# Index scores of three blocks summed by sign diagonals on TensorE, with the threshold search and the value GEMM beside them

## The chip, the cores and the metric

The kernel runs on one core of a Trainium2 chip. The metric is the device time of one execution in microseconds (us). A core has five engines with queues of their own: TensorE (PE; its weight loads are listed as PEld), VectorE (DVE), ScalarE (ACT), GpSimd (POOL) and SyncE (SP, which issues the DMA transfers). An engine works its queue off in order. They wait for each other through semaphores alone.

## What is computed

The program is a two-layer decoder trunk in float32 on 1,040 positions (16 meta tokens and 1,024 tokens, width 1,024). The change touches the first layer's sparse attention. For each block of 128 queries an indexer scores all earlier keys, the 256 best keys of each query stay, and grouped attention (16 query heads, 4 key heads) runs over them:

```
q, k, v, qi, ki, wi = split(h @ w_in)         # 1024, 256, 256, 512, 64, 8 columns
logits = einsum('qhd,sd->qhs', qi_blk, ki)    # 8 index heads of 64
score  = einsum('qh,qhs->qs', w_blk, relu(logits))
score  = where(causal, score, -inf)
_, idx = top_k(score, 256)                    # per query row
s = einsum('qgrd,qkgd->qgrk', q_blk, k[idx]) * scale ; p = softmax(s) ; o = p @ v[idx]
```

After it come the output projection, an MLP, a second attention layer over a shared key and value set, and another MLP. They are the same before and after.

## The kernel before

**Index scores.** A block b of 128 queries has L[b] = 144 + 128 b keys: 272, 400, 528, 656, 784, 912, 1,040 for b = 1 to 7 (block 0 keeps all its keys). `scores(b)` (L452) walks over 8 heads and, in each, over chunks of at most 400 keys: two matmuls (L458, L459; operand format float32r, high and low part of the key) make the logits in a PSUM bank of the tag `pt`, ScalarE takes relu times the absolute head weight (L461, tile `tm`), and VectorE multiplies by the sign of the weight and adds to the score row `sc` (L463 for head 0, L465 for the others). For b = 5, 6, 7 these are 2, 3 and 3 chunks times 8 heads, 64 pieces. Over all of them the moving columns are 8 x (784 + 912 + 1,040) = 21,888.

**Threshold search.** `threshold(b0, b1)` (L483) finds each row's 256th value bit by bit: 31 bits, and in a bit one count per block. VectorE counts blocks 1, 2, 5 and 7 (L481, a comparison with an accumulator); ScalarE counts 3, 4 and 6 (L498, Sign with an accumulator). Then three small VectorE operations form the next candidate `cand` (L500, L503, L504), for which the next bit's counts wait. After the bits there is a last count, and one `mask` (L521) for each block: a count, a comparison (L526), a scan (L527), two combining operations (L529, L531) and two GpSimd operations. `thr1` searches blocks 1 to 4 (37 steps), `thr2` blocks 5 to 7 (36 steps).

**GEMMs.** `a_gemm` (through `gemm_c`, L192) makes K in 2 and Q in 8 slices of 128 columns. A slice has three chunks of some 346 positions, a chunk 24 matmuls (L199). Each K chunk goes through a head norm (L264: ScalarE L269, L279, L284; a float32 matmul L274; VectorE L286 to L292) and through `rope` (L355: four DMAs, three GpSimd operations). A Q chunk takes two ScalarE copies (L437 and one at L141) and rope. `gemm_v` (L213) makes V in 9 windows of 24 matmuls with 256 columns (L220). The copied pieces lie in a ring `raw` of five tiles (L375).

**Stages.** `weave` (L226) hands out the steps of several generators in proportion to their weights: first scores of 5 to 7, the K GEMM and 4 steps of `thr1` (L558); then 29 steps of `thr1`, 16 of `thr2` and the Q GEMM (L561); then the last 4 of `thr1` and V (L563). After that comes the attention of this layer: `unit(b, g)` makes logits (L671), their biased minimum on VectorE (L674) and the exponential (L699). `pv_stream` (L713) transposes the probabilities (L725) two units later and multiplies them with V. `WHOLE` (L707) says for each block how many of 8 such products are done in one float32 matmul (L745, recorded as two); the others are split into a high and a low float32r part (a VectorE subtraction at L148, two matmuls at L748). One step of `thr2` goes with each unit of blocks 0 to 4 (L767). The weave is no fixed order: when the program is built, a scheduler orders each engine's queue, with the order of the weave as priority, and lets an operation whose inputs it expects earlier go ahead.

## Time and profile before

| | us |
|---|---|
| median of three runs | 2957.9 (2950.74 to 2958.91) |
| profiled execution, its own time | 2962.78 |
| span of the trace in it | 2960.6 |
| TensorE busy | 2727.7 (92%) |
| VectorE busy | 2092.8 (71%) |
| ScalarE busy | 1485.5 (50%) |
| GpSimd busy | 1307.6 (44%) |

The busy times are sums over the whole program, whose stages have different limits. The change lies in the first quarter: scores of the large blocks with K at about 131 to 190 us, Q to 314, V to 352, attention of blocks 0 to 4 from 358 to 525, of blocks 5 to 7 to 686. Everything after that, three quarters of the time, is the same code in both. In the rows below "x" counts instructions, a mean is in ns, and a granted clock of 1.00 is 2.4 GHz, 0.50 is 1.2 GHz. A float32 matmul is recorded as two instructions.

### The profile page before, as it was taken

The page shows a single profiled execution, that of the slowest core. Times are in us where ns is not written, and L with a number is a line of the kernel's source. Part 1 is how long each engine was busy: PE and PEld are TensorE (multiplying, and loading weights), DVE is VectorE, ACT ScalarE, POOL GpSimd, SP SyncE. Part 2 cuts the span into 40 slices and gives each one's busy share as a digit, 9 for nine tenths or more (in the row PEclk, how much of TensorE's full clock was granted, in tenths as well). Part 3 has the DMA queues.
Part 4 walks back from the last instruction along what each step waited for, and adds up shares of the span by engine and source line. Part 5 has one row for each costly group of instructions (what it writes and reads, how often), then busy time and mean ns, then how long its engine had stood idle before and what let it go on. Part 6 is the DMA issues. An engine that isn't in the chain of part 4 may idle for free.

```text
span 2960.6 us, 45611 instructions
## 1 busy us (share of the span) xinstructions
PE 2727.7 (92%) x16570; PEld 2384.1 (81%) x16570; DVE 2092.8 (71%) x3802; ACT 1485.5 (50%) x2828; POOL 1307.6 (44%) x1199
## 2 busy tenths in 40 slices
...
GB/s 170 79 46 73 53 16 1 1 1 99 81 80 158 144 144 187 144 123 131 152 63 59 51 51 51 51 51 51 102 58 68 116 162 149 152 185 150 150 134 73
DMA packets 243154, 281.92 MB, mean 95 GB/s; under 512 B 22273, under 2 KB 183873, under 8 KB 242929
## 3 DMA queue, kind: packets, MB, share of 16 engines
...
## 4 chain that ended last, share of the span: by engine, by line
PE 58%; DVE 22%; DMA 7%; ACT 5%; POOL 4%; issue 4%; SPq 0%; DVEq 0%; POOLq 0%; ACTq 0%
PE ac L986 32%; PE ps L186 6%; PE ps L199 6%; DMA ld<-rdr 5%; DVE sc L481 4%; PE ps L671 2%; PE ps L1330 2%; PE ps L725 2%; PE ps L745 2%; PE ps L1308 2%; PE ps L1276 1%; PE ps L748 1%; DVE sc L465 1%; DVE opa L148 1%; DVE opc L148 1%
## 5 line engine op out<-in xcount | busy, mean ns | idle before, releaser
L986 PE MATMUL ac<-opc,g 128*128 128x260 f32 (+1 forms) x3456 | 580.4, 324 | 33.3 <-ACT q L141 11.5
L986 PEld LDWEIGHTS ac<-opc,g 128*128 128x128 f32 x3456 | 504.9, 191 | 92.7 <-issue 13.4
L986 PE MATMUL ac<-opb,g 128*128 128x260 f32 (+1 forms) x2304 | 389.6, 325 | 55.1 <-ACT opb L141 38.2
L986 PEld LDWEIGHTS ac<-opb,g 128*128 128x128 f32 x2304 | 336.8, 191 | 99.0 <-ACT opb L141 43.8
L986 PE MATMUL ac<-opa,g 128*128 128x260 f32 (+1 forms) x2304 | 394.6, 324 | 1.3 <-ACT g L141 0.8
L986 PEld LDWEIGHTS ac<-opa,g 128*128 128x128 f32 x2304 | 340.3, 191 | 37.2 <-ACT g L141 1.0
L978 POOL TENSOR_TENSOR t<-rb,t 128x512 f32<-128x512 f32 x128 | 191.4, 1495 | 338.4 <-DMA rb<-in_mlp_w_dram 288.7
L148 DVE TENSOR_TENSOR g<-t,g 128x512 fp32r<-128x512 f32 x256 | 225.9, 882 | 132.0 <-ACT g L141 129.6
L141 ACT ACTIVATE g<-t 128x512 fp32r<-128x512 f32 x256 | 161.1, 629 | 264.9 <-PE ac L986 166.9
L199 PE MATMUL ps<-xhb,wh 128*128 128x256 f32 (+5 forms) x640 | 207.4, 324 | 5.0 <-DVE z L1138 2.9
L199 PE MATMUL ps<-xhb,wl 128*128 128x256 f32 (+5 forms) x640 | 196.6, 307 | 0.0
L199 PE MATMUL ps<-xlb,wh 128*128 128x256 f32 (+5 forms) x640 | 196.4, 307 | 0.0
L978 POOL TENSOR_TENSOR t<-ra 128x512 f32<-128x512 f32 x64 | 96.3, 1504 | 177.1 <-DVE g L148 172.0
L1290 POOL TENSOR_SCALAR bp<-bp,bnm 128x400 f32<-128x400 f32 (+7 forms) x128 | 108.5, 858 | 143.8 <-DVE bnm L1288 143.6
L148 DVE TENSOR_TENSOR g<-rb,g 128x512 fp32r<-128x512 f32 x128 | 114.6, 896 | 57.0 <-ACT g L141 56.9
L671 PE MATMUL ps<-ks,qs 128*128 128x512 f32 (+4 forms) x448 | 130.0, 396 | 20.8 <-DVE qs L602 12.5
L141 ACT ACTIVATE bth<-ps 128x512 fp32r<-128x512 f32 (+4 forms) x224 | 110.9, 498 | 60.8 <-PE ps L1308 54.6
L199 PEld LDWEIGHTS ps<-xhb,wh 128*128 128x128 f32 x640 | 121.9, 190 | 23.6 <-issue 9.3
L141 ACT ACTIVATE q<-ac 128x520 f32<-128x520 f32 (+1 forms) x96 | 57.6, 600 | 165.4 <-PE ac L986 163.0
L1330 PE MATMUL ps<-bth,bvs 128*128 128x512 f32 (+2 forms) x420 | 135.6, 399 | 3.5 <-DVE qb L1337 2.7
L148 DVE TENSOR_TENSOR bth<-ps,bth 128x512 fp32r<-128x512 f32 (+4 forms) x210 | 119.1, 568 | 26.0 <-ACT bth L141 24.7
L1267 POOL TENSOR_SCALAR bp<-bcb,cq 128x144 f32<-128x144 f32 (+7 forms) x128 | 101.3, 794 | 77.7 <-DMA bcb<-cdr 47.7
...
## 6 DMA issues: line engine op xcount, KB each, us to landing
...
```

What stands on the lines that cost most here:

```text
L141: nc.scalar.activation(dst, src, AF.Copy, scale=scale)
L148: (nc.gpsimd if pool else nc.vector).tensor_tensor(lo, src, f32(hi), OP.subtract)
L186: nc.tensor.matmul(o[0:n, 0:m], a[:, k, 0:n], b[:, k, s:s + m], start=(k == 0 and j == 0), stop=(k == NK - 1 and j == 2))
L199: nc.tensor.matmul(o[0:n, 0:m], a[:, k, 0:n], b[:, k, s:s + m], start=(k == 0 and j == 0), stop=(k == NK - 1 and j == 2))
L481: nc.vector.tensor_scalar(eqb[:, 0:L[b]], scs(b), th, None, op, OP.add, accum_out=dst[:, b:b + 1])
L671: nc.tensor.matmul(o, qs[:, h, :], kc, start=(v == 0), stop=(v == 1))
L725: nc.tensor.transpose(pt[0:rows, j * n:j * n + n], pr[j][q0:P, c0:c0 + rows], ident[q0:P, q0:P])
L978: nc.gpsimd.tensor_tensor(t, a, c, OP.subtract)
L986: nc.tensor.matmul(t[:, i, 0:m], a[:, j, :], c[:, j, o:o + m], start=start and j == 0 and v == 0, stop=stop and j == 3 and v == 2, skip_gr ...
L1267: nc.gpsimd.tensor_scalar(pj, cb[:, 0:n], 1.0, cq[:, b, h:h + 1], OP.mult, OP.add)
L1290: nc.gpsimd.tensor_scalar(pr[i], pr[i], nm[:, 3, i:i + 1], 0.0, OP.mult, OP.add)
L1330: nc.tensor.matmul(po[:, j0 * P:], v_kb, th[0:rows, v, j0 * P:], start=(kb == 0 and v == 0), stop=(kb == last and v == 1))
```

## The change

Scores of blocks 5, 6 and 7 come from a new `scores_pe`. For each block GpSimd builds eight diagonal matrices `dg` that hold the signs of the weights, with one affine_select of 128x1024. Chunks are now the outer loop and heads the inner one. For each head TensorE makes the logits as before, ScalarE the relu as before, and TensorE then adds the head into a PSUM bank with a float32 matmul of `dg` and `tm`, two heads later. At a chunk's end ScalarE copies the sum to `sc`; in a block's last chunk VectorE adds the causal triangle to the last 128 columns. The 64 operations of L463 and L465 of these blocks are gone.

Beside these scores now run K, the whole V GEMM and 30 steps of `thr1`; beside Q run the other 7 of `thr1`, its masks among them, and 26 steps of `thr2`. The third weave is gone. The `raw` ring has four tiles, which makes room for `dg`. In blocks 5 to 7 no product of probabilities and V is whole any more: 24 of 96 were, 18 of them with 512 columns.

```diff
-THR_Q = 16
-T1 = 4
+THR_Q = 26
+T1 = 30
...
-            return iw.tile([P, HWID], F32, tag="raw", name=f"raw_{name}_{s}", bufs=5)
+            return iw.tile([P, HWID], F32, tag="raw", name=f"raw_{name}_{s}", bufs=4)
...
+        def scores_pe(b):
+
+            sb = scs(b)
+            t0 = NMETA + P * b
+            dg = iw.tile([P, IH, P], F32, tag="dg", name=f"dg{b}", bufs=1)
+            sg = wsg[:, b].rearrange("p (h o) -> p h o", o=1).to_broadcast([P, IH, P])
+            nc.gpsimd.affine_select(out=dg, in_=sg, pattern=[[0, IH], [-1, P]], compare_op=OP.is_equal, fill=0.0,
+                                    base=0, channel_multiplier=1)
+            for s, m in chunks_of(L[b]):
+                acc = bank("ps")
+                tms = {}
+
+                def add(h):
+                    nc.tensor.matmul(acc[:, 0:m], dg[:, h], tms.pop(h)[:, 0:m], start=h == 0, stop=h == IH - 1)
+                for h in range(IH):
+                    o = bank("pt")
+                    nc.tensor.matmul(o[:, 0:m], s3[:, h, t0:t0 + P], kih[:, s:s + m], start=True, stop=False)
+                    nc.tensor.matmul(o[:, 0:m], s3[:, h, t0:t0 + P], kil[:, s:s + m], start=False, stop=True)
+                    tms[h] = tm = iw.tile([P, 400], F32, tag="tm", name=f"tm{b}_{h}_{s}", bufs=3)
+                    nc.scalar.activation(tm[:, 0:m], o[:, 0:m], AF.Relu, scale=wab[:, b, h:h + 1])
+                    if h > 1:
+                        add(h - 2)
+                    if h < IH - 1:
+                        yield
+                add(IH - 2)
+                add(IH - 1)
+                e = m - P if s + m == L[b] else m
+                if e > 0:
+                    copy(sb[:, s:s + e], acc[:, 0:e])
+                if e < m:
+                    nc.vector.tensor_tensor(sb[:, s + e:s + m], acc[:, e:m], trifar, OP.add)
+                yield
...
-        weave((chain(*[scores(b) for b in range(5, NB)]), 12),
-              (chain(*[a_gemm(QW + mi * P, P, k_evac(mi), fine=True) for mi in range(2)]), 18),
+        weave((chain(*[scores_pe(b) for b in range(5, NB)]), 64),
+              (chain(*[a_gemm(QW + mi * P, P, k_evac(mi), fine=True) for mi in range(2)],
+                     gemm_v(w_in, QW + KW, xh, xl, v_evac)), 27),
               (islice(thr1, T1), T1))
-        weave((islice(thr1, 33 - T1), 33 - T1), (islice(thr2, THR_Q), THR_Q),
+        weave((thr1, 37 - T1), (islice(thr2, THR_Q), THR_Q),
               (chain(*[a_gemm(mi * P, P, q_evac(mi), fine=True) for mi in range(QW // P)]), 72))
-        weave((thr1, 4), (gemm_v(w_in, QW + KW, xh, xl, v_evac), 9))
...
-        WHOLE = (6, 6, 6, 6, 6, 2, 2, 2)
+        WHOLE = (6, 6, 6, 6, 6, 0, 0, 0)
```

The scheduler's order decides where the steps of the search come to stand. On VectorE, just ahead of the attention, the queue before has bits of `thr2` (784 and 1040 are the counts of blocks 5 and 7), the last V split, and then the key and query stacks `ks` and `qs`, with the first attention operation (L674) in the last row:

```order
L503 TENSOR_TENSOR dlt<-cnt,lim 128x3
L504 SCALAR_TENSOR_TENSOR cand<-dlt,flip 128x3
L500 TENSOR_SCALAR flip<-cand 128x3
L481 TENSOR_SCALAR sc,cnt<-sc,cand 128x784
L148 TENSOR_TENSOR wl_6810<-wr_6808,wh_6809 128x1024
L481 TENSOR_SCALAR sc,cnt<-sc,cand 128x1040
L148 TENSOR_TENSOR va<-ps_3578,va 16x4x64
L148 TENSOR_TENSOR ks_3643<-ka,ks_3643 64x272 x4
L602 TENSOR_TENSOR qs_3641<-qa,qs_3641 64x8x128
L603 TENSOR_TENSOR qs_3641<-qa,qs_3641 64x8x128
L148 TENSOR_TENSOR ks_3643<-ka,ks_3643 64x240 x2
L674 ISA pb_3630,nm_0_3661<-ps_3662,sc,s_99 128x144
```

At the same place the changed queue has the last mask's last operation (1040, L564, which was L531), the scales `s` of the logits, and then the same stacks:

```order
L564 SCALAR_TENSOR_TENSOR sc<-sc,cand 128x1040
L255 TENSOR_TENSOR s_99<-s_99 128x144
L148 TENSOR_TENSOR wl_7055<-wr_7053,wh_7054 128x1024
L256 TENSOR_TENSOR s_99<-s_99 128x144
L257 TENSOR_SCALAR s_99<-s_99 128x144
L258 TENSOR_TENSOR s_99<-s_99 128x144
L602 TENSOR_SCALAR s_99<-s_99 128x144
L603 TENSOR_SCALAR s_99<-s_99 128x144
L656 MEMSET pm 16x384
L148 TENSOR_TENSOR ks_3725<-ka,ks_3725 64x272 x4
L635 TENSOR_TENSOR qs_3723<-qa,qs_3723 64x8x128
L636 TENSOR_TENSOR qs_3723<-qa,qs_3723 64x8x128
```

So the changed queue holds all 31 bits of `thr2`, its last count and its three masks ahead of the first attention operation, and none behind it. The queue before holds 20 of the 31 bits there (19 whole ones and the counts of the 20th); the other 11, the last count and the masks stand between attention operations. Of `thr1`'s 31 bits, 4 stood in the queue ahead of the end of the large blocks' scores; now 29 do.

On TensorE, where the large blocks' scores begin, the queue before has only logits (`ps<-kih,qis`) between GEMM matmuls:

```order
L199 MATMUL ps_1342<-xh,wl_1338 128x348
L458 MATMUL ps_1352<-kih,qis 128x392
L459 MATMUL ps_1352<-kil,qis 128x392
L458 MATMUL ps_1358<-kih,qis 128x392
L459 MATMUL ps_1358<-kil,qis 128x392
L458 MATMUL ps_1364<-kih,qis 128x392
```

The changed queue adds a diagonal matmul (`tm`, `dg`) two heads behind the logits, so TensorE now waits there for ScalarE's `tm`:

```order
L487 MATMUL ps_1372<-kih,qis 128x392
L488 MATMUL ps_1372<-kil,qis 128x392
L199 MATMUL ps_1357<-xh,wh_1352 128x348
L484 MATMUL ps_1338<-tm_0_0_1342,dg_1336 128x392
L487 MATMUL ps_1385<-kih,qis 128x392
L488 MATMUL ps_1385<-kil,qis 128x392
L484 MATMUL ps_1338<-tm_1_0_1370,dg_1336 128x392
L199 MATMUL ps_1357<-xl,wh_1352 128x348
```

On ScalarE in the middle of these scores, the queue before has relus (L461) and a piece of a head norm:

```order
L461 ACTIVATE tm_5_696_1951<-ps_1948,wab 128x344
L269 ACTIVATE sc<-ps_1890 128x346
L461 ACTIVATE tm_6_0_1973<-ps_1970,wab 128x348
L461 ACTIVATE tm_6_348_1979<-ps_1976,wab 128x348
L461 ACTIVATE tm_6_696_1985<-ps_1982,wab 128x344
L461 ACTIVATE tm_7_0_1991<-ps_1988,wab 128x348
L461 ACTIVATE tm_7_348_1997<-ps_1994,wab 128x348
```

The changed queue has Sign counts of blocks 3 and 4 (L531, which was L498), which wait for VectorE's `cand`, between the relus (L490), and a copy of the summed scores (L141):

```order
L531 ACTIVATE sc,cnt<-sc,cand 128x656
L141 ACTIVATE sc<-ps_1725 128x304
L531 ACTIVATE sc,cnt<-sc,cand 128x528
L490 ACTIVATE tm_0_608_1861<-ps_1858,wab 128x304
L490 ACTIVATE tm_1_608_1873<-ps_1870,wab 128x304
L269 ACTIVATE sc<-ps_1798 128x346
L490 ACTIVATE tm_2_608_1886<-ps_1883,wab 128x304
L531 ACTIVATE sc,cnt<-sc,cand 128x656
L490 ACTIVATE tm_3_608_1899<-ps_1896,wab 128x304
L490 ACTIVATE tm_4_608_1905<-ps_1902,wab 128x304
```

## Rows read from the trace of the kernel before

**Rows 1.** Busy time of each engine in stretches of the span: the columns are the stretch in us, its length, PE, PEld, DVE, ACT and POOL busy us with instruction counts, the mean granted clock of TensorE, the DMA share and GB/s.

```profile
131.00:190.00 59.00, 50.85 (x287) 44.68 (x287) 58.70 (x124) 45.44 (x100) 20.29 (x17) 1.00 0.13 34
190.00:352.00 162.00, 142.46 (x908) 139.13 (x906) 156.03 (x400) 100.25 (x220) 85.43 (x89) 0.90 0.21 54
358.00:390.00 32.00, 26.52 (x89) 17.24 (x90) 24.59 (x82) 21.99 (x67) 13.99 (x21) 0.50 0.22 51
390.00:430.00 40.00, 36.43 (x166) 21.80 (x165) 35.71 (x112) 30.04 (x83) 14.27 (x22) 0.68 0.05 13
430.00:480.00 50.00, 47.11 (x252) 32.42 (x250) 44.57 (x124) 43.23 (x102) 23.28 (x29) 1.00 0.00 1
480.00:525.00 45.00, 39.34 (x183) 26.49 (x184) 39.21 (x75) 28.89 (x61) 22.53 (x24) 0.89 0.00 1
525.00:686.00 161.00, 156.90 (x872) 115.31 (x871) 119.50 (x260) 121.11 (x241) 59.29 (x54) 1.00 0.01 1
```

**Rows 2.** Groups of VectorE instructions by line, 131 to 192 us: the sums of the scores.

```profile
L465 DVE SCALAR_TENSOR_TENSOR sc<-tm,wsg,sc 128x304 f32<-128x304 f32 (+3 forms) x56 | 34.1, 653 | 0.0
...
L463 DVE TENSOR_SCALAR sc<-tm,wsg 128x304 f32<-128x304 f32 (+3 forms) x8 | 4.7, 591 | 0.0
```

**Rows 3.** Instructions of TensorE in order of time (start us, us until the last one ends): two neighbouring float32r matmuls of V with 256 columns; then in the attention one whole product (a float32 matmul of 512 columns, two records), what follows it, one split product (two float32r matmuls of 512 columns), and what follows that.

```profile
310.73 0.28 PE L220 MATMUL ps<-wl,xh 128*128 128x256 f32 x1
310.85 0.28 PE L220 MATMUL ps<-wh,xh 128*128 128x256 f32 x1
...
642.87 1.02 PE L745 MATMUL ps<-th,va 128*128 128x512 f32 x2
643.73 0.60 PE L725 MATMUL ps<-ident,pb 128*128 128x128 f32 x4
644.09 0.71 PE L748 MATMUL ps<-th,va 128*128 128x512 f32 x2
644.64 0.62 PE L671 MATMUL ps<-ks,qs 128*128 128x512 f32 x2
```

**Rows 4.** Groups of ScalarE instructions by line, 131 to 192 us: the Sign counts of the search and the reads of their accumulators.

```profile
L498 ACT ACTIVATE sc<-sc,cand 128x528 bf16<-128x528 f32 (+1 forms) x10 | 7.9, 792 | 1.9 <-DVE cand L504 1.9
...
L498 ACT ACTIVATION_READ_ACCUMULATOR sc<-sc,cand 128x1 f32 x9 | 1.8, 202 | 0.0
```

**Rows 5.** VectorE in order of time: in the Q stage the two counts of a `thr1` bit, and two of the small operations; near the end of V the first count of a `thr2` bit and the first count of the next one.

```profile
201.73 0.48 DVE L481 TENSOR_SCALAR_CACHE_REDUCE sc<-sc,cand 128x272 f32<-128x272 f32 x1
...
202.26 0.63 DVE L481 TENSOR_SCALAR_CACHE_REDUCE sc<-sc,cand 128x400 f32<-128x400 f32 x1
...
202.81 1.33 DVE L503 TENSOR_TENSOR dlt<-cnt,lim 128x3 int32<-128x3 f32 x1
...
205.06 0.85 DVE L500 TENSOR_SCALAR flip<-cand 128x3 int32<-128x3 int32 x1
...
343.20 1.02 DVE L481 TENSOR_SCALAR_CACHE_REDUCE sc<-sc,cand 128x784 f32<-128x784 f32 x1
...
346.14 1.02 DVE L481 TENSOR_SCALAR_CACHE_REDUCE sc<-sc,cand 128x784 f32<-128x784 f32 x1
```

**Rows 6.** Groups of VectorE instructions by line, 190 to 352 us: the three small operations of the search, the weight splits and the V splits.

```profile
L504 DVE SCALAR_TENSOR_TENSOR cand<-dlt,flip 128x4 int32<-128x4 int32 (+1 forms) x47 | 20.2, 430 | 1.6
L503 DVE TENSOR_TENSOR dlt<-cnt,lim 128x4 int32<-128x4 f32 (+1 forms) x46 | 17.7, 384 | 0.5 <-ACT sc L498 0.2
L500 DVE TENSOR_SCALAR flip<-cand 128x4 int32<-128x4 int32 (+1 forms) x47 | 16.2, 346 | 1.5
...
L148 DVE TENSOR_TENSOR wl<-wr,wh 128x1024 fp32r<-128x1024 f32 x3 | 4.1, 1380 | 0.0
L148 DVE TENSOR_TENSOR va<-ps,va 128x256 fp32r<-128x256 f32 x8 | 3.3, 414 | 0.0
```

**Rows 7.** Who waited for whom (us in total, times, longest): two waits of TensorE at 131 to 190 us, one of ScalarE at 190 to 352 us.

```profile
PE ps L458 <- DVE ln L287: 5.8, 5, 3.1
...
PE ps L458 <- ACT tm L461: 2.3, 4, 1.2
...
ACT sc L498 <- DVE cand L504: 43.8, 25, 4.5
```

**Rows 8.** Groups of VectorE instructions by line, 358 to 525 us, those of the search: counts, scan, the two combining operations, the comparison, and one candidate update at the end of the bits.

```profile
L481 DVE TENSOR_SCALAR_CACHE_REDUCE sc<-sc,cand 128x784 f32<-128x784 f32 (+2 forms) x28 | 32.3, 1154 | 0.2
...
L527 DVE TENSOR_TENSOR_SCAN sc<-sc 128x784 f32<-128x784 f32 (+2 forms) x3 | 6.2, 2057 | 0.0
...
L531 DVE SCALAR_TENSOR_TENSOR sc<-sc,cand 128x784 f32<-128x784 f32 (+2 forms) x3 | 4.6, 1518 | 0.0
...
L529 DVE SCALAR_TENSOR_TENSOR sc<-sc,cnt 128x784 f32<-128x784 f32 (+2 forms) x3 | 3.7, 1248 | 0.0
...
L526 DVE TENSOR_SCALAR sc<-sc,cand 128x784 f32<-128x784 f32 (+2 forms) x3 | 2.1, 699 | 0.0
...
L514 DVE CUSTOM_DVE_ANT_0 cand<-cand,one 128x6 uint16<-128x6 uint16 x1 | 1.9, 1852 | 0.0
```

**Rows 9.** VectorE in order of time: the last split of V, and the first operation of the attention.

```profile
352.52 0.41 DVE L148 TENSOR_TENSOR va<-ps,va 16x256 fp32r<-16x256 f32 x1
...
358.08 0.37 DVE L674 CUSTOM_DVE_ANT_0 pb<-ps,sc,s 128x144 f32<-128x144 f32 x1
```

**Rows 10.** VectorE by line, 525 to 686 us: the subtraction of the split products.

```profile
L148 DVE TENSOR_TENSOR th<-ps,th 128x512 fp32r<-128x512 f32 (+1 forms) x75 | 48.1, 655 | 17.6 <-ACT th L141 16.9
```

## The prediction

> **What bounds the kernel now.** I read the busy time by stretch first [rows 1]. While the large blocks' scores run (131 to 190 us) VectorE is busy for 58.7 of 59.0 us, and through Q and V (190 to 352) for 156.0 of 162. TensorE is idle for 8 and 20 us there, ScalarE for 14 and 62. So VectorE sets the end of these two stretches. In the attention of blocks 0 to 4 (358 to 525) no engine is full: VectorE is busy for 144.1 of 167 us (24.6, 35.7, 44.6 and 39.2), TensorE for 149.4 (26.5, 36.4, 47.1 and 39.3). The latter runs partly at a low clock: the granted clock is 0.50 in the first 32 us, 0.68 in the next 40, then 1.00 and 0.89. In blocks 5 to 7 (525 to 686) TensorE is busy for 156.9 of 161 us at 1.00 and is the bound. I count from 131 us to the start of the attention, from there to block 5, and then the tail; the rest of the program is unchanged.
>
> **Stage 1, scores with K, V and most of `thr1`.** It loses VectorE's 34.1 + 4.7 = 38.8 us of sums [rows 2]. TensorE gets them back as float32 matmuls. Its sum goes by moving columns. A float32r matmul of 256 columns is followed by the next one 0.12 us later [rows 3], 0.469 ns a column. K has 6 chunks x 24 x 347 = 49,920 columns, the logits 2 x 21,888 = 43,776, V 9 x 24 x 256 = 55,296: 148,992 columns, 69.9 us. A float32 product of 512 columns occupies TensorE from 642.87 to 643.73 [rows 3], 1.68 ns a column: 36.8 us for the 21,888 columns of the diagonals and 3.5 us for the six head norms (2,080). Sum **110 us**.
>
> ScalarE: the 45.4 us of the old stretch [rows 1] hold nearly all relus, K's head norms and 10 Sign counts. 29 bits of two counts are 58, so 48 more at 0.79 + 0.20 [rows 4], 47.5 us. V's nine splits, two weight copies and eight copies of sums are 19 operations of at most about 0.79: up to 15, taken as 8. Sum 101. VectorE: 58.7 - 38.8, plus 25 more bits at about 2.25 (1.08 for both counts, from 201.73 to 202.81 [rows 5], and 0.43 + 0.38 + 0.35 for the small ones [rows 6]), plus V's 6: 82 us, no longer full.
>
> So TensorE sets this stage, with ScalarE close behind, and a diagonal matmul now waits for ScalarE's relu, whose queue also holds Signs that wait for `cand`. Behind that matmul stand the next logits and the GEMMs. The trace has TensorE waiting 5.8 + 2.3 = 8.1 us in the old stage [rows 7]; I add that much: **118 us**, between 110 and 135 (every wait of ScalarE below exposed as well). It ends at 249.
>
> Small edits cost nothing by their cover. The three sign tables stand on GpSimd behind rope, and the first diagonal stands two heads (118 / 64 x 2 = 3.7 us) behind its block's first logits; the nearest row is VectorE's split of the same 128x1024 at 1.38 us [rows 6]; uncovered, three times twice that would be 8 us, inside the bounds. Four raw tiles hold four chunks of some 6 us each in the next stage. On SP the two weight loads of V pass Q's; the DMA share is 0.13 and 0.21 [rows 1].
>
> A rule weighed against this: the product of 512 float32 columns takes 0.86 us here [rows 3]. The Trainium skill (TensorE: Matmul & The Clock Gate, section "Back-to-back issue gap") gives a gap of columns / 2.4 + 2.5 ns for a matmul and no dearer one for float32. By that the 64 diagonals would be an estimate of 64 x 145 ns = 9.3 us and stage 1 would fall to ScalarE's 101; the row speaks against it.
>
> **Stage 2, Q with the rest of the search.** The weave's numbers leave 10 steps of `thr2` to the attention, but VectorE's queue has every bit and mask ahead of the first attention operation, so all of it must end first. From the 156.0 us of 190 to 352 [rows 1] I take 25 bits of `thr1` (56) and V's splits and their weights (3.3 + two of 1.38 [rows 6], 6). I add 11 bits of `thr2` at 3.5 (38.5), and the last count and masks: scan 6.2, combining 4.6 + 3.7, comparison 2.1, update 1.9, six counts at 1.154 [rows 8], 25.4. Two counts (2 us) go before the end of stage 1. Sum **156 us**; I take **154**, since old leftovers of scores and K sit in the 156.0. The price of 3.5: one bit with nothing beside it takes 2.94 (343.20 to 346.14 [rows 5]), of which the counts are about 2.4 (1.02 for 784 elements, to scale for 1,824) and the small operations 0.55. Their means over the stage sum to 1.16, and single ones reach 1.33 and 0.85 between GpSimd's ropes [rows 5, 6]. Bounds: 2.94 and 3.6 for all 31 bits, 137 to 160. Q's own matmuls (8 x 24 x 1,040 columns x 0.469 = 94 us) lie beside it; the queues tie them to the search through ScalarE.
>
> It ends at 403. From V's last split to the first attention operation pass 5.6 us [rows 9], so the attention starts at 409 and not at 358: **+51**.
>
> **The attention of blocks 0 to 4** loses the search: of VectorE's 144.1 us, 32.3 + 6.2 + 4.6 + 3.7 + 2.1 + 1.9 = 50.8 in the large rows alone [rows 8]. What is late next is TensorE. Its busy time at the lower of the two levels is worth 26.5 x 0.50 + 36.4 x 0.32 + 39.3 x 0.11 = 29 us if all were granted at 2.4 GHz, and its idle time is 17.6. The ends are 0 (TensorE's own chain rules and stays slow) and 47 us. The first 32 us show TensorE busy at 0.50 while VectorE has room, so I expect the start to stay slow: 14 of the idle time and 13 of the clock, **-27**.
>
> **The tail.** 18 products go from 0.86 to 0.55 us (644.09 to 644.64 [rows 3]): -5.6. VectorE gets 18 x 0.66 = 12 us more [rows 10] on 119.5 of 161. I take **-5**, between -6 and +6.
>
> **Sum**: 51 - 27 - 5 = **+19 us**. The profiled execution took 2962.8 us (span 2960.6), so 2982 there; it lies 4.9 above the median, which gives **2977**.
>
> **Rivals.**
> A, on the other side: GpSimd's interference leaves VectorE. The ropes spread over a longer stage, a bit costs 2.94 and without the wait inside it about 2.8, so stage 2 loses 31 x 0.7 = 22 us, the masks some 4, and stage 1, whose TensorE waits come mostly from VectorE's late head norms (5.8 of 8.1 us), runs in 110: 19 - 22 - 4 - 8 = -15, hence **2943**. It needs a bit under 2.95 to turn the sign. For it: fewer small operations (33 triples against 47). Against: GpSimd's work per chunk is the same.
> B: the attention gives all of its 47 us back, because VectorE's pauses were what kept TensorE slow: 19 - 20 = -1, **2957**. For it: 1.00 at 430 to 480. Against: 0.50 with VectorE 77% busy.
> C: stage 1 runs in lockstep. ScalarE waits 43.8 us for `cand` in the old Q stage [rows 7]; if such waits hold up relus and with them TensorE, and its clock falls to the lower level for a part, the stage takes 150: **3009**. For it: relus and Signs alternate in the queue. Against: two relus lie in most gaps.
> D: a float32 pass costs what the rule above says: 118 falls to 101, **2960**. Only the page speaks for it.
> That the search is not moved is no rival: the queues show it.
>
> **How the numbers follow.** Forecast 0.58, A 0.12, B 0.14, C 0.12, D 0.04. The forecast's own range, from the bounds of the four terms added as independent ones (about 10, 11, 12 and 5 us), is 2957 to 2997. Below 0.3% (9 us) a measurement of this kernel can't tell from no change. Faster: A and a little of B, 0.15. Same: the rest of B, D and the forecast's lowest tenth, 0.25. Slower: the rest, 0.60. To hold 8 in 10 the range goes halfway into A and to the start of C: 2946 to 3004.
>
> **What would show it.** Right: stage 1 near 118 us with TensorE nearly full and VectorE idle by a third; the first attention operation near 409; VectorE full ahead of it and TensorE with gaps; blocks 0 to 4 in about 140 us; the tail some 5 us shorter. Wrong: a stage 1 beyond 135 (C); 31 bits at less than 3 us each (A); blocks 0 to 4 near 120 (B). Attention operations ahead of the masks would overturn the whole sum.

## The result, and the profile after

The changed kernel takes 2999.5 us (median of 4 runs, 2998.38 to 3003.04), the kernel before beside it 2958.4 (2950.74 to 2959.56): a ratio of 1.0142, 95% interval 1.0122 to 1.0163, so about 41 us slower. The profiled executions have spans of 2996.4 and 2960.6 us.

Three marks on VectorE serve for every kernel below: A, the first attention operation; B, the first biased minimum of block 5 (784 wide), where blocks 0 to 4 end; C, the first split for the output projection, where the tail ends. Behind C stands the same code everywhere; it took between 2264.8 and 2276.6 us over the profiles here, with no order in it, so parts are compared by the marks (whose start, at 131 us, itself moves by some us between executions) and whole kernels by their ratio.

| | A | A to B | B to C | C | C to the end |
|---|---|---|---|---|---|
| before | 358.1 | 169.9 | 157.8 | 685.9 | 2274.7 |
| changed | 423.1 | 153.0 | 154.6 | 730.6 | 2265.7 |

Up to C the change costs 44.8 us; 9.0 of it don't show in the spans, because the unchanged rest of this execution was that much shorter.

Busy time by stretch in the changed kernel, in the columns of [rows 1]: the scores with K, V and 29 bits of `thr1`; Q with the rest of the search; the preparation of the attention; blocks 0 to 4 in four pieces; the tail.

```profile
131.00:245.00 114.00, 109.65 (x613) 90.84 (x612) 72.62 (x255) 93.58 (x220) 21.95 (x23) 1.00 0.08 20
245.00:411.00 166.00, 126.70 (x717) 124.31 (x715) 158.40 (x312) 67.09 (x129) 89.59 (x87) 0.80 0.21 55
411.00:423.00 12.00, 1.13 (x4) 0.93 (x4) 10.16 (x14) 5.11 (x10) 6.32 (x7) 0.50 0.34 90
423.00:455.00 32.00, 26.36 (x100) 17.42 (x101) 20.44 (x77) 22.77 (x68) 14.21 (x21) 0.50 0.21 50
455.00:495.00 40.00, 35.80 (x188) 23.98 (x188) 22.58 (x81) 28.25 (x81) 15.93 (x24) 0.80 0.01 1
495.00:545.00 50.00, 49.41 (x265) 34.74 (x263) 30.08 (x83) 41.16 (x98) 26.95 (x30) 1.00 0.00 1
545.00:576.00 31.00, 29.60 (x161) 20.49 (x159) 17.31 (x42) 23.15 (x50) 13.22 (x14) 1.00 0.00 1
576.00:731.00 155.00, 148.69 (x855) 114.49 (x854) 127.96 (x281) 120.02 (x236) 56.53 (x53) 0.99 0.01 1
```

TensorE is nearly full in the first (109.65 of 114) and VectorE in the second (158.40 of 166; in [rows 1] it was full in both). In the preparation TensorE has 1.13 us of work. Blocks 0 to 4 begin with 32 us at 0.50, as before, and then TensorE is nearly full at 0.80 and 1.00 while VectorE has room.

The search in the second stretch, by line of VectorE, as in [rows 6]: the counts, then the three small operations.

```profile
L514 DVE TENSOR_SCALAR_CACHE_REDUCE sc<-sc,cand 128x784 f32<-128x784 f32 (+4 forms) x80 | 86.6, 1082 | 1.5
L536 DVE TENSOR_TENSOR dlt<-cnt,lim 128x3 int32<-128x3 f32 (+1 forms) x33 | 13.5, 408 | 3.3 <-ACT raw_q L141 0.5
...
L533 DVE TENSOR_SCALAR flip<-cand 128x3 int32<-128x3 int32 (+1 forms) x32 | 11.5, 360 | 0.9
L537 DVE SCALAR_TENSOR_TENSOR cand<-dlt,flip 128x3 int32<-128x3 int32 (+1 forms) x33 | 11.0, 332 | 0.9
```

Who waited for whom from 245 to 423 us, as in [rows 7]:

```profile
ACT sc L531 <- DVE cand L537: 65.2, 26, 5.2
POOL sc L565 <- DVE sc L564: 30.4, 6, 9.4
...
PE ps L447 <- ACT sc L437: 26.2, 7, 5.7
...
PE ps L704 <- DVE qs L635: 23.8, 1, 23.8
```

ScalarE waits 65.2 us for `cand` (43.8 in the Q and V stretch before), and behind its Signs stand Q's copies: TensorE waits 26.2 us for those. GpSimd waits 30.4 us for masks. TensorE waits 23.8 us for the first query stack (L704), before which it last had Q.

What came last ahead of A, in GpSimd's order of time: the last mask's two operations, then the last rotation of Q.

```profile
413.47 1.06 POOL L565 TENSOR_SCALAR sc<-sc 128x1040 f32<-128x1040 f32 x1
414.62 0.45 POOL L566 TENSOR_TENSOR sc<-sc,tri 128x128 f32<-128x128 f32 x1
415.03 0.86 POOL L361 TENSOR_TENSOR rotq<-rotq,rs 128x346 f32<-128x346 f32 x1
415.86 0.79 POOL L362 TENSOR_TENSOR raw_q<-raw_q,rc 128x346 f32<-128x346 f32 x1
416.73 0.91 POOL L363 TENSOR_TENSOR qa<-raw_q,rotq 128x346 f32<-128x346 f32 x1
```

And ScalarE's next two operations, the key and query stacks, with what released the first:

```profile
417.68 1.78 ACT L141 ACTIVATE ks<-ka 64x272 fp32r<-64x272 f32 x4 [8.08 <-POOL qa L363]
419.48 2.13 ACT L141 ACTIVATE qs<-qa 64x1024 fp32r<-64x1024 f32 x2
```

The last mask leaves VectorE at 410.5, but Q's last rotation stood behind its two GpSimd operations and ends at 417.6; only then do the stacks begin, and the attention 5.4 us after that.

### The profile page after: what moved, and what is told of

Same layout as the page of the kernel before. It is cut to its first block, busy times and chain, and to the rows that moved or that the text cites. A ratio compares the mean times of both kernels' runs of the same rounds, so it can differ in the third digit from the quotient of the medians.

```text
span 2996.4 us, 45902 instructions
## 1 busy us (share of the span) xinstructions
PE 2751.3 (92%) x16698; PEld 2413.5 (81%) x16698; DVE 2058.9 (69%) x3762; ACT 1490.2 (50%) x2836; POOL 1317.2 (44%) x1202
## 4 chain that ended last, share of the span: by engine, by line
PE 61%; DVE 17%; ACT 6%; DMA 6%; POOL 4%; issue 4%; SPq 0%; DVEq 0%; ACTq 0%; POOLq 0%
PE ac L1019 32%; PE ps L199 7%; PE ps L186 6%; DMA ld<-rdr 5%; DVE sc L514 3%; PE ps L704 2%; PE ps L1363 2%; PE ps L758 2%; PE ps L1341 2%; PE ps L1309 2%; PE ps L781 2%; PE ps L778 1%; DVE g L148 1%; DVE opa L148 1%; DVE opc L148 1%
## 5 line engine op out<-in xcount | busy, mean ns | idle before, releaser
L1019 PEld LDWEIGHTS ac<-opc,g 128*128 128x128 f32 x3456 | 505.6, 192 | 88.5 <-ACT q L141 12.8
L141 ACT ACTIVATE g<-t 128x512 fp32r<-128x512 f32 x256 | 161.1, 629 | 265.0 <-PE ac L1019 154.4
L704 PE MATMUL ps<-ks,qs 128*128 128x512 f32 (+4 forms) x448 | 129.0, 392 | 26.7 <-DVE qs L635 23.8
L141 ACT ACTIVATE bth<-ps 128x512 fp32r<-128x512 f32 (+4 forms) x224 | 111.3, 499 | 59.9 <-PE ps L1341 53.6
L141 ACT ACTIVATE q<-ac 128x520 f32<-128x520 f32 (+1 forms) x96 | 57.6, 600 | 165.7 <-PE ac L1019 163.3
L141 ACT ACTIVATE wh<-wr 128x1024 fp32r<-128x1024 f32 (+1 forms) x84 | 87.4, 1041 | 103.8 <-PE ps L186 70.7
```

Of the source, the lines that this page charges most:

```text
L141: nc.scalar.activation(dst, src, AF.Copy, scale=scale)
L704: nc.tensor.matmul(o, qs[:, h, :], kc, start=(v == 0), stop=(v == 1))
L1019: nc.tensor.matmul(t[:, i, 0:m], a[:, j, :], c[:, j, o:o + m], start=start and j == 0 and v == 0, stop=stop and j == 3 and v == 2, skip_gr ...
```

## The experiments

All marks and times, where a ratio was measured with its 95% interval (to the kernel before on the same chip), else the time of one execution. e7 and e12 compute the scores less precisely and e8 and e11 leave Q unrotated: they price a term and are no candidates.

| | A | A to B | B to C | time |
|---|---|---|---|---|
| e1 scores only | 393.5 | 166.8 | 153.6 | 1.0080 [1.0050, 1.0109] |
| e2 weave only | 417.6 | 147.2 | 154.6 | 1.0110 [1.0087, 1.0133] |
| e3 V last | 417.0 | 147.2 | 153.6 | 1.0088 [1.0064, 1.0112] |
| e4 block 7 | 383.7 | 160.0 | 153.6 | 1.0033 [1.0019, 1.0048] |
| e5 gate | 401.1 | 171.1 | 153.4 | 1.0118 [1.0093, 1.0143] |
| e6 gate, mixed | 396.0 | 171.6 | 153.5 | 1.0122 [1.0098, 1.0146] |
| e7 one pass | 423.3 | 150.7 | 153.5 | 2995.0 |
| e8 less rotation | 404.1 | 151.8 | 154.6 | 2979.8 |
| e9 block 7, gate | 384.3 | 171.1 | 153.8 | 1.0064 [1.0046, 1.0083] |
| e10 masks off GpSimd | 420.0 | 151.9 | 153.9 | 2994.9 |
| e11 before, less rotation | 345.3 | 170.0 | 157.8 | 2947.4 |
| e12 gate, one pass | 389.6 | 171.3 | 153.4 | 2984.4 |
| e13 gate, no Sign | 388.3 | 180.6 | 153.4 | 3000.7 |
| e14 ring and split | 358.2 | 169.0 | 153.5 | 0.9979 [0.9964, 0.9993] |
| e15 fill | 370.7 | 169.3 | 158.1 | 1.0008 [0.9994, 1.0022] |
| e16 fill and split | 370.1 | 164.7 | 153.6 | 0.9986 [0.9972, 1.0000] |
| e17 no queue ties | 388.5 | 182.4 | 153.5 | 2995.0 |

**The two halves apart.** In the diffs of the weaves here, K GEMM and Q GEMM stand for the chains of `a_gemm` that the change's diff shows. e1 is the changed kernel with the old order:

```diff
-THR_Q = 26
-T1 = 30
+THR_Q = 16
+T1 = 4
...
+        weave((chain(*[scores_pe(b) for b in range(5, NB)]), 64), (K GEMM, 18), (islice(thr1, T1), T1))
+        weave((islice(thr1, 33 - T1), 33 - T1), (islice(thr2, THR_Q), THR_Q), (Q GEMM, 72))
+        weave((thr1, 4), (gemm_v(w_in, QW + KW, xh, xl, v_evac), 9))
```

> The changed kernel with the old weaves: the three blocks' scores on TensorE, but K alone beside them with 4 bits of thr1, V last again, and (by the order of VectorE's queue) 21 of 31 bits of thr2 ahead of the attention, the rest and the masks inside it. Theory 1 (TensorE's added columns lengthen the stage in which it is nearly full, and VectorE cannot use the time that it is given): the large scores take 84 to 92 us instead of 59, Q and V stay at about 162 because VectorE stays full there, the first attention operation comes at about 387 instead of 358, the attention of blocks 0 to 4 stays at 170; about 2984 us. Rival (the sums leave VectorE for little, and only the moved search costs): the large scores stay near 65 us, VectorE takes the search earlier, the attention starts at 358 or before; 2955 us or less.

e2 has the new order with VectorE's sums:

```diff
-        weave((chain(*[scores_pe(b) for b in range(5, NB)]), 64),
+        weave((chain(*[scores(b) for b in range(5, NB)]), 12),
```

> The changed kernel with the three blocks' scores summed on VectorE as before: the new weaves, the four raw tiles and the split products alone. Theory 1: VectorE is full in the first stage, 58.7 us of old work and 25 more bits of thr1 at 2.25 and V's splits, so that stage takes about 121 us against the changed kernel's 114, the rest is as in the changed kernel; about 3006 us, so the sign diagonals gain some 7 us within the new weave. Rival (the diagonals cost more on TensorE than the sums on VectorE whatever stands beside them): the stage takes 100 us or less and the kernel 2985 us.

Each half alone loses: at B e1 is 32.3 us late and e2 36.7, both together 48.0. The first stretches, of e1 and then of e2:

```profile
131.00:215.00 84.00, 82.55 (x393) 64.96 (x392) 23.59 (x65) 51.89 (x111) 20.20 (x20) 1.00 0.08 20
215.00:393.00 178.00, 150.34 (x942) 147.52 (x940) 165.69 (x409) 105.84 (x226) 86.34 (x90) 0.86 0.21 56
```

```profile
131.00:234.00 103.00, 79.28 (x483) 71.88 (x484) 100.51 (x316) 88.83 (x211) 20.95 (x21) 0.93 0.10 26
```

e1 is theory 1's case: TensorE full for 84 us where the stretch was 61, VectorE idle for 60 of them because its queue has only four bits there. Q and V then took 173 us and not the 162 that I expected; why is open. In e2 the stage ends at 233.6, neither at 252 as I expected nor at 231: VectorE is full, but the stage holds less than I summed (I had taken 2.25 us a bit from the Q stage; GpSimd is busy for only 20.95 of 103 us here). So within the new order the diagonals, not the sums, are the slower way in this stage: 114 us against 103. At A 5.5 of the 11 us are left. Another 5.8 at B are no price of the diagonals but one of TensorE's clock (shown at the end of this section), and the ratios of the two kernels, 1.0110 and 1.0142, have intervals that overlap. The expected gain of 7 was wrong in sign.

**Where V stands.** e3 takes V back to the end:

```diff
-              (chain(K GEMM, gemm_v(w_in, QW + KW, xh, xl, v_evac)), 27), (islice(thr1, T1), T1))
-        weave((thr1, 37 - T1), (islice(thr2, THR_Q), THR_Q), (Q GEMM, 72))
+              (K GEMM, 18), (islice(thr1, 22), 22))
+        weave((thr1, 15), (islice(thr2, 20), 20), (Q GEMM, 72))
+        weave((islice(thr2, 6), 6), (gemm_v(w_in, QW + KW, xh, xl, v_evac), 9))
```

> The changed kernel with V at the end again, beside the masks of thr2, and 22 steps of thr1 in the first stage; all 31 bits and the masks stay ahead of the attention by VectorE's queue. In the changed kernel 12.6 us pass from the last mask to the first attention operation, and TensorE idles for 23.8 us before it. Theory 1 (V used to hide the scales' small operations and the last rope): this preparation falls to about 6 us; the first stage falls to about 95 us, its 8 missing bits lengthen the next by 18; the first attention operation comes at about 412 instead of 423, and the whole takes about 2988 us. If TensorE's work just ahead also raises its clock in the first 32 us of the attention (0.50 in both kernels), some 10 us more, 2978. Rival (the preparation is VectorE's own work and lies on the path wherever V stands): 423 stays within 3 us and the time within 5 of the changed kernel's.

The total came out as expected (2958.4 x 1.0088 = 2984), but A only half: 417. From the last mask (403.5) to A 13 us still pass, now with V's last window, two weight splits and the stacks in a row on ScalarE. The scales went out of the way; the preparation did not shrink. So the total was right partly by luck: blocks 0 to 4 took 147.2 us instead of 153.0 and made up for it.

**Balance, and the search put back.** e4 has block 7 alone by diagonals in the old order:

```diff
+T1 = 10
...
+        weave((chain(scores(5), scores(6), scores_pe(7)), 32), (K GEMM, 18), (islice(thr1, T1), T1))
```

> The old weaves with 10 instead of 4 steps of thr1 beside the scores, block 7 alone summed by diagonals (24 of 64 pieces), blocks 5 and 6 on VectorE. Theory 1 (time is worth moving only as far as the two engines balance): TensorE's 14 us more and VectorE's 15 us less put both near 68 us in the first stage, Q and V lose the 6 bits, 13 us; the attention starts some 5 us earlier than in the kernel before, the tail gains 3; about 2950 us. Rival (any diagonal on TensorE costs more than its sum on VectorE saves): the attention starts at 358 or later; 2960 us or more.

A came 26 us late, so the rival was right in sign. VectorE's queue had 28 counts of `thr2` ahead of the attention instead of 20, which blurs the reason; e9, below, takes these 8 away. In e5 a dependency keeps the search where it was:

```diff
-THR_Q = 26
+THR_Q = 20
...
+        gz = att_in.tile([P, 1], F32, name="gz", bufs=1)
+        nm0 = []
...
+                if b0 == 5 and bit == 11:
+                    nc.vector.tensor_scalar(gz, nm0[0][:, 1, 0:1], 0.0, None, OP.mult)
+                    nc.vector.tensor_scalar(lim[:, bs], lim[:, bs], gz, None, OP.add)
...
+            nm0.append(nm)
...
-            if b < 5:
+            if 0 < u < 20:
                 n = min(THR_A[b], 36)
```

> The changed kernel with one added dependency: the 20th bit of thr2 (its limits) waits for the first attention unit, so that VectorE's queue again holds 20 counts of thr2 ahead of the attention and 11 bits, the last count and the three masks inside it. Theory 1 (the loss is the part of the search that left the attention, where VectorE had room for it, for a stage in which VectorE is full): the stage after the scores loses about 41 us of bits and 25 of masks on VectorE and becomes as long as Q on TensorE allows, 105 to 115 us; the attention starts at about 361 instead of 423, blocks 0 to 4 take about 168 again instead of 153, the tail stays; about 2955 us, level with the kernel before. Rival (the sign diagonals and the merged Q stage cost that much themselves, the place of the search little): the attention starts at 390 or later and the kernel takes 2980 us or more.

Theory 1 fell here: 401, not 361, and the rival's numbers came out. With 22 us won at A and 18 lost up to B, where the search stands was worth 4 us. The stretches of e5: scores, search beside Q, Q alone, preparation:

```profile
131.00:245.00 114.00, 108.75 (x608) 90.24 (x609) 73.87 (x257) 95.56 (x224) 21.98 (x23) 1.00 0.09 24
245.00:340.00 95.00, 77.60 (x435) 75.68 (x434) 90.14 (x190) 38.33 (x74) 46.32 (x48) 0.84 0.23 58
340.00:393.00 53.00, 47.00 (x290) 46.74 (x288) 9.86 (x18) 15.25 (x30) 37.17 (x38) 0.87 0.26 68
393.00:401.00 8.00, 1.13 (x4) 0.93 (x4) 6.23 (x10) 5.11 (x10) 2.47 (x3) 0.50 0.53 136
```

VectorE is done at 340 and idle from there (9.86 of 53), and Q still needs 53 us. Beside the search TensorE was busy for only 77.6 of 95 us, at a mean clock of 0.84. Something had held Q back while the search ran. e6 moves block 5's sums to VectorE in it:

```diff
-(chain(*[scores_pe(b) for b in range(5, NB)]), 64)
+(chain(scores(5), scores_pe(6), scores_pe(7)), 52)
```

> The same with block 5's scores summed on VectorE as before, blocks 6 and 7 by diagonals. Theory 1: VectorE, idle for some 41 us of the first stage's 114, takes 16 sums (10 us) and TensorE loses 6,272 float32 columns (10.5 us): the stage takes about 104 us, everything behind it moves up by as much; about 2946 us. Rival (ScalarE's relus and Signs, busy for 93.6 us, or their waits set the stage): 111 us or more, no gain over the run with three blocks on TensorE.

The scores end at 240.9 instead of 246.6, between theory 1 and the rival, and A comes 5.1 us earlier: half of what TensorE lost in columns. The whole time doesn't show it (1.0122 and 1.0118). e9 is e4 with e5's dependency:

> The run with block 7 alone by diagonals, with the added dependency that keeps 20 counts of thr2 ahead of the attention (28 there without it). Theory 2 (both engines carry the program up to block 5, so a move pays only while neither is full; the 8 bits that went ahead cost that run 3.6 us each): VectorE loses 29 us ahead of the attention, which starts at 358 to 365 instead of 384, and takes 168 to 171 us instead of 160; about 2955 us, level with the kernel before. Rival (TensorE's 14 us more bound it): the attention starts at 375 or later, 2970 us or more.

The rival's number, though not for its reason: A at 384.3, and from 131 to there TensorE was busy for 212 us of 253 and VectorE for 213. Neither is full. The scores end at 206.0 instead of 191.8, which is 14 of the 26 us; what the other 12 wait for was not separated.

**What a float32 pass is worth.** e7 and e12 are the changed kernel and e5 with this:

```diff
-            dg = iw.tile([P, IH, P], F32, ...
+            dg = iw.tile([P, IH, P], F32R, ...
-                    tms[h] = tm = iw.tile([P, 400], F32, ...
+                    tms[h] = tm = iw.tile([P, 400], F32R, ...
```

> The changed kernel with diagonals and relu tiles in float32r, so that a diagonal is one pass of 0.47 ns a column; the scores lose their low bits before the sum. Theory 1 (the first stage is TensorE's sum): its 21,888 columns fall from 36.8 to 10.3 us, TensorE stops being the bound and the stage falls from 114 to about 98, held by ScalarE's 93.6; the rest as in the changed kernel, some 16 us off the start of the attention, from 423 to about 407. Rival (the stage is ScalarE's and its waits): 110 us or more.

> The run with the added dependency and three blocks by diagonals (attention at 401), with diagonals and relu tiles in float32r, one pass of 0.47 ns a column (the scores lose their low bits). Theory 2 (with the search back in the attention TensorE is the bound ahead of it, while in the changed kernel VectorE was and one pass gained nothing): TensorE loses 26 us less its pauses, the attention starts at 380 to 388. Rival (the queues tie the engines together, whichever is full): 396 or later.

e7, the scores and all from there to A:

```profile
131.00:240.00 109.00, 90.60 (x559) 82.44 (x558) 75.62 (x257) 92.91 (x221) 24.27 (x24) 0.95 0.10 26
240.00:423.00 183.00, 128.26 (x714) 125.73 (x712) 174.09 (x325) 71.80 (x138) 95.33 (x93) 0.76 0.21 55
```

TensorE loses 19 us in the first stretch, which ends 5.1 us earlier, and A stays at 423: VectorE, busy for 75.62 + 174.09 of the 292 us, takes it back. Its operations `dlt` and `cand` took 495 and 429 ns on average behind the scores, where the changed kernel has 408 and 332; why is open. The rival was right; the float32 passes were not what the changed kernel waited for. In e12, with the search put back, A gains 11.5 us and comes at 389.6, just behind theory 2's 380 to 388. All of the gain is there by the end of the scores (235.2 instead of 246.6); from there to A both take 154 us.

**GpSimd beside VectorE.** e8 (of the changed kernel) and e11 (of the kernel before):

```diff
-            nc.gpsimd.tensor_tensor(rot, rot, sn, OP.mult)
-            nc.gpsimd.tensor_tensor(src, src, c, OP.mult)
+            if not name[0] == "q" or name[1] == "i":
+                nc.gpsimd.tensor_tensor(rot, rot, sn, OP.mult)
+                nc.gpsimd.tensor_tensor(src, src, c, OP.mult)
```

> The changed kernel with GpSimd's two multiplications in the rotation of Q left out (48 of 72 operations there; Q is then not rotated). Theory 1 (VectorE's small operations are slow beside GpSimd's): the three small ones of a bit, 0.41, 0.36 and 0.33 us in the changed kernel, fall to about 0.25 each, the bits of thr2 from about 3.7 to 3.2 us, and the masks' rows too; Q's last rotation also ends sooner behind the masks; the first attention operation moves from 423 to about 403. Rival (the small operations are slow for their semaphores, not for GpSimd): their means stay above 0.33 and the attention starts at 418 or later.

> The kernel before with GpSimd's two multiplications in the rotation of Q left out (Q is then not rotated). Theory (GpSimd's operations slow VectorE's small ones, in this kernel too, where VectorE bounds Q and V): the three small operations, 0.43, 0.38 and 0.35 us over 47 bits, fall to about 0.22 each, 23 us, of which TensorE, busy for 142 of 162, lets some 14 be seen: the attention starts at about 344 instead of 358. Rival (they hide behind TensorE there): 355 or later.

A came as forecast in both: at 404.1 (403 expected) and at 345.3 (344 expected). The rows of e8, same lines and stretch as above (shifted by one):

```profile
L515 DVE TENSOR_SCALAR_CACHE_REDUCE sc<-sc,cand 128x784 f32<-128x784 f32 (+4 forms) x80 | 86.6, 1083 | 1.5
...
L537 DVE TENSOR_TENSOR dlt<-cnt,lim 128x3 int32<-128x3 f32 (+1 forms) x33 | 9.8, 298 | 3.3 <-ACT raw_q L141 0.5
L538 DVE SCALAR_TENSOR_TENSOR cand<-dlt,flip 128x3 int32<-128x3 int32 (+1 forms) x33 | 7.9, 241 | 0.9
L534 DVE TENSOR_SCALAR flip<-cand 128x3 int32<-128x3 int32 (+1 forms) x32 | 6.7, 210 | 0.9
```

The counts are unchanged (1082 and 1083 ns); the small operations fall from 408, 360 and 332 to 298, 210 and 241. From 131 us to A VectorE's busy time falls from 241.2 to 223.8 us, and A moves by 19.0: the last mask by 15.3 (410.5 to 395.2), and the preparation behind it, where Q's rotations are shorter now, by 3.7. In e11 the three operations fell from 384, 430 and 346 ns (`dlt`, `cand`, `flip`) to 313, 252 and 240.

**The preparation.** e10:

```diff
-            nc.gpsimd.tensor_scalar(sb, rank[:, 0:n], -NEG, NEG, OP.mult, OP.add)
-            nc.gpsimd.tensor_tensor(sb[:, n - P:], sb[:, n - P:], tri, OP.add)
+            if b < 5:
+                nc.gpsimd.tensor_scalar(sb, rank[:, 0:n], -NEG, NEG, OP.mult, OP.add)
+                nc.gpsimd.tensor_tensor(sb[:, n - P:], sb[:, n - P:], tri, OP.add)
+            else:
+                nc.scalar.activation(sb, rank[:, 0:n], AF.Copy, scale=-NEG, bias=NEG)
+                nc.vector.tensor_tensor(sb[:, n - P:], sb[:, n - P:], tri, OP.add)
```

> The changed kernel with GpSimd's two operations of each thr2 mask on ScalarE (the fill) and VectorE (the triangle). In the changed kernel these stand in GpSimd's queue ahead of Q's last rotations, wait for VectorE's masks, and the last rotation ends at 417.6, 7 us behind the last mask. Theory (this queue is what makes the preparation 12.6 us long): the last rotation ends by about 405, the small operations of the scales run without GpSimd beside them, and the attention starts at 415 to 418 instead of 423. Rival (the preparation is the scales, copies and stacks themselves): 421 to 424.

From the last mask (413.5) to A 6.5 us pass instead of 12.6, and Q's last rotation ends at 412.2, ahead of the mask; but VectorE now ends 3 us later, for the triangles and for other operations that go ahead (a weight split and a part of the scales, which stood behind the mask before), and A is at 420.0, between theory and rival. So the queue is shown to cost 3 us at A; the other 3 of the 6.1 us now pass ahead of the last mask.

**Who holds Q.** e13 is e5 with this:

```diff
-ACT_SET = (3, 4, 6)
+ACT_SET = (3, 4)
```

> The run with the added dependency (attention at 401), with block 6 counted on VectorE like blocks 5 and 7, so that no Sign of thr2 stands in ScalarE's queue. There Q's first 16 pieces took 6.7 us each beside the search and the last 7, with no search left, 4.5. Theory 3 (Signs that wait for VectorE's candidate hold up Q's copies behind them, and so Q runs at the search's pace): VectorE gets 20 counts of 912, about 23 us more, in a stage in which it is idle for 34 of its last 40 us; Q's pieces take about 4.8 us each throughout, and the attention starts at 366 to 376. Rival (Q's pace is TensorE's clock, the rotations or the ring): 392 or later.

Q's first nine pieces took 4.5 us each, as theory 3 says; of the others four took 10.6 to 13.1. The waits from 245 to 388:

```profile
ACT raw_q L141 <- POOL qa L363: 48.2, 11, 9.4
POOL sc L570 <- DVE sc L569: 42.2, 4, 17.7
```

GpSimd stood 42.2 us at four mask operations, with Q's rotations behind them; the ring filled, and ScalarE stood 48.2 us for a free tile. A is at 388.3, between theory 3 and the rival, and the whole is no faster, since block 6's counts now stand on VectorE in the attention too (180.6 us for blocks 0 to 4 instead of 171.1). e17 is e13 with this:

```diff
-            nc.gpsimd.tensor_scalar(sb, rank[:, 0:n], -NEG, NEG, OP.mult, OP.add)
-            nc.gpsimd.tensor_tensor(sb[:, n - P:], sb[:, n - P:], tri, OP.add)
+            nc.vector.tensor_scalar(sb, rank[:, 0:n], -NEG, NEG, OP.mult, OP.add)
+            nc.vector.tensor_tensor(sb[:, n - P:], sb[:, n - P:], tri, OP.add)
```

> The run with block 6 counted on VectorE (attention at 388), and the two GpSimd operations of every mask on VectorE as well. In that run Q's first 9 pieces took 4.5 us each and then stalled: GpSimd waited 42.2 us in four pieces for VectorE's masks of thr1, with Q's rotations behind these waits, until the ring of four tiles was full (ScalarE waited 48.2 us for it). Theory 3, completed (Q is tied to the search by the heads of two in-order queues, ScalarE's Signs and GpSimd's mask operations): Q's pieces take about 4.7 us throughout and end by about 360; VectorE, with some 120 us of work, ends about there, and the attention starts at 366 to 374. Rival (VectorE's work alone sets the stage and the ties don't matter): 385 or later.

Its stretches (scores; Q; the end of the search; what follows), and one wait of SP's queue from 245 to 388:

```profile
131.00:245.00 114.00, 109.64 (x617) 91.20 (x616) 72.52 (x256) 94.80 (x223) 22.63 (x22) 1.00 0.08 20
245.00:350.00 105.00, 105.00 (x704) 105.00 (x702) 102.41 (x205) 30.02 (x59) 73.12 (x70) 1.00 0.30 76
350.00:374.00 24.00, 1.04 (x8) 0.87 (x8) 22.54 (x52) 1.34 (x4) 0.00 (x0) 0.57 0.10 29
374.00:388.00 14.00, 0.77 (x4) 0.77 (x4) 3.97 (x7) 4.75 (x9) 7.78 (x9) 0.50 0.40 102
```

```profile
SPq L160 <- DVE sc L611: 30.3, 1, 30.3
```

Q now takes 105 us, with TensorE and VectorE both full (105.00 and 102.41) and the clock at 1.00. Its last piece is copied at 350, and VectorE is done at 374. But A is at 388.5: a weight load of the output projection stands in SP's queue, held by VectorE until 369.9 (a weight split ends then, as does the copy that the profile names), with the last 12 rotation transfers behind it. So theory 3 was right on Q and wrong on A, where the rival had the number and a part of the reason. VectorE's end at 374 and 5.6 us for the stacks give 380 as an estimate; the 9 us beyond that are those of a third in-order queue.

**Ring, split products and the clock.** e14 is the kernel before with two small edits:

```diff
-name=f"raw_{name}_{s}", bufs=5)
+name=f"raw_{name}_{s}", bufs=4)
-        WHOLE = (6, 6, 6, 6, 6, 2, 2, 2)
+        WHOLE = (6, 6, 6, 6, 6, 0, 0, 0)
```

> The kernel before with two parts of the change alone: four raw tiles instead of five, and all products of blocks 5 to 7 split. By the prediction the ring costs nothing (attention at 358 within 2 us) and the tail falls by some 4 us, from 157.9 to about 154: about 2955 us. Rival (the ring was the unseen cost of the Q stage): Q's pieces come later and the attention starts at 364 or later, 2965 us.

A at 358.2, the tail 153.5: the ring costs nothing there, and the split products gain 4.3 us. It is the one version whose interval lies below the kernel before, by 0.07 to 0.36%.

e15 and e16 (with the second edit of e14) add matmuls behind V:

```diff
+        fill = bank("pt")
+        for _ in range(40):
+            nc.tensor.matmul(fill, va[:, 6, 0, :], va[:, 6].rearrange("p g d -> p (g d)"), start=True, stop=True)
```

> The kernel before with 40 more matmuls of 512 columns, whose result nobody reads, between V and the attention, where TensorE is idle for 12.5 us and after which it has a granted clock of 0.50 for some 32 us. Theory 4 (this low clock follows the pause, and the attention's first blocks are bound by TensorE at that clock): the clock stays at 1.00 into the first units, the attention of blocks 0 to 4 takes some 155 to 160 us instead of 170, about 2947 us. Rival (the pauses of the first units themselves lower the clock, or VectorE bounds them): 0.50 again, 168 to 172 us, and 2958 us; if the 40 take longer than the pause, a few us more.

> The same with all products of blocks 5 to 7 split, as in the changed kernel: by theory 4 and the tails of all runs so far some 4 us less than that, about 2943 us, faster than both kernels; by the rival 2954 us.

No gain: the rivals' numbers came out, but theory 4 was not tested, since the pause was not closed. e15 by stretch, and TensorE in order of time:

```profile
346.00:352.00 6.00, 5.49 (x43) 4.53 (x42) 5.76 (x16) 2.58 (x5) 0.07 (x1) 1.00 0.01 3
352.00:358.00 6.00, 6.00 (x29) 4.92 (x28) 5.69 (x17) 3.39 (x6) 0.00 (x0) 1.00 0.00 1
358.00:364.00 6.00, 2.60 (x12) 1.90 (x11) 5.84 (x12) 5.76 (x14) 0.00 (x0) 0.94 0.54 141
364.00:370.00 6.00, 0.92 (x4) 0.72 (x4) 5.75 (x9) 5.82 (x9) 0.00 (x0) 0.50 0.53 123
370.00:380.00 10.00, 7.80 (x31) 5.79 (x32) 9.38 (x39) 6.91 (x25) 3.13 (x8) 0.50 0.44 109
380.00:390.00 10.00, 10.00 (x38) 6.71 (x38) 6.75 (x27) 7.32 (x23) 4.21 (x7) 0.50 0.00 0
390.00:400.00 10.00, 8.96 (x63) 6.29 (x63) 6.63 (x23) 6.87 (x20) 6.18 (x9) 0.50 0.18 54
```

```profile
353.69 6.73 PE L566 MATMUL ps<-va 128*128 128x512 f32 x29
363.82 1.10 PE L674 MATMUL ps<-ks,qs 128*128 128x144 f32 x4 [3.40 <-DVE qs L605]
371.22 1.10 PE L674 MATMUL ps<-ks,qs 128*128 128x144 f32 x4 [6.30 <-DVE nm L677]
```

The clock stays at 1.00 through the 40 matmuls. But everything in front came later (the scores end at 196.2 instead of 191.8, V's last split at 360.3 instead of 352.5), and TensorE still waits 3.4 us for the query stack and then 6.3 for VectorE; from 364 to 400 it is at 0.50, though busy for most of that.

What the low clock costs blocks 0 to 4 can be read from other runs. From A to B the changed kernel, e2, e7, e8 and e10 have the same instructions in the same order on all four engines, and still take 153.0, 147.2, 150.7, 151.8 and 151.9 us. From A to B in these five, in that order:

```profile
423.07:576.04 152.97, 141.21 (x707) 96.67 (x707) 90.41 (x280) 115.30 (x293) 70.36 (x88) 0.84 0.05 11
417.59:564.77 147.18, 134.10 (x707) 91.91 (x708) 90.49 (x281) 114.98 (x293) 70.39 (x88) 0.90 0.05 12
423.25:573.96 150.71, 138.06 (x707) 94.40 (x707) 90.39 (x280) 115.38 (x293) 70.36 (x88) 0.87 0.05 11
404.10:555.88 151.78, 139.56 (x707) 95.25 (x707) 90.39 (x280) 115.13 (x293) 70.11 (x88) 0.86 0.05 12
419.99:571.87 151.88, 139.81 (x707) 95.12 (x708) 90.30 (x281) 115.46 (x293) 70.15 (x88) 0.86 0.05 11
```

The busy times of the other engines agree within half a us, and TensorE's fall in the order of the granted clock, from 0.84 to 0.90. The changed kernel and e2 are even alike in the first 20 us behind A (TensorE busy for 14.86 us in both, at 0.50); then the clock rose 21.5 us behind A in e2 and 40.8 in the changed kernel, and the 5.8 us between them are all there by the 32nd of the 80 minima. So TensorE at the lower level does cost the first blocks time: 5.8 us for some 19 us more of it. Why the clock rose earlier in one is open, and single profiles differ by that much at B without any difference in the code.

## Why the prediction was wrong

The sign was right, and the steps came in the order forecast, but the forecast of 2977 was 22 us short: +19 was forecast and +41 measured. The time lies in the stated range only because that was stretched to the start of rival C; the forecast's own 2957 to 2997 misses it. What limits each stage came out as argued; three terms were mis-sized, one of them for a queue that was overlooked. By its own steps:

| step | forecast | measured |
|---|---|---|
| stage 1 | 118 | 114.2 (131 to 245.2) |
| stage 2 | 154 | 165.3 (to 410.5, the last mask) |
| preparation | 5.6 | 12.6 |
| start of the attention | +51 | +65.0 |
| blocks 0 to 4 | -27 | -17.0 |
| tail | -5 | -3.2 |
| sum | +19 | +44.8 |

- **Stage 1** held: TensorE at 109.65 for a sum of 110, VectorE idle by a third. That TensorE *sets* the stage is only partly shown. With 26 us of passes gone (e7, e12) it ended 5 to 11 us earlier, so something stands just behind, ScalarE and the waits by the sums; that it is they was not tested. Rival D's 101 would have been too low a bound, and its gain would have been taken back (e7).
- **Stage 2 is the step that failed**: "Sum 156 us; I take 154". It added VectorE's busy time, and the stage took 165.3. VectorE was busy for 158.4 us of the 166 in the rows, near the sum of 156, but 7.6 more passed in small pauses, most of them between dependent operations (3.3 in front of `dlt`, 1.5 in front of the counts, 0.9 for each of the others in the rows above). [rows 1] has 6 us of such idle time in the Q and V stretch before (156.03 of 162); a sum that starts from the busy time leaves them out, and I took another 2 off. The upper bound, 160, had no room for them either. GpSimd's interference did not leave: `dlt`, `flip` and `cand` took 1.10 us together against 1.16 before, and with two thirds of its operations gone the last mask comes 15.3 us earlier (e8). So rival A is out.
- **The preparation** was taken from [rows 9], where V stood between Q's last rotation and the attention: 12.6 us for 5.6. I had asked what stands behind a moved step on VectorE and ScalarE, but not in GpSimd's queue, where Q's last rotation now stands behind the last mask. e10 takes that away and has 6.5 us, of which 3 are a gain at A.
- **Blocks 0 to 4.** Of the 27, 14 were idle time of TensorE and 13 its clock. Measured over A to B, its busy time fell by 11.2 us (152.4 to 141.2) and its idle time by 5.7 (17.5 to 11.8). So the term of the idle time was the wrong one: VectorE's pauses were a smaller part of TensorE's than I took, and rival B, which gave them all of it, was further off. In e2, with the same instructions, the clock rose earlier and the stretch is 22.7 us shorter than before instead of 17.0: of the 10 us missed, 5.8 are the clock's timing in this execution.
- **The tail**: -3.2 for -5; e14 puts the split products alone at -4.3.
- "The queues tie them to the search through ScalarE" stood in the prediction without a price. e5, e13 and e17 show that ScalarE's, GpSimd's and SP's queues each do. That is the mechanism of rival C, in the other stage (stage 1, at 114 us, shows nothing of C's 150): Q's pieces took 6.4 us in the changed kernel, 5.2 before, and 4.4 in e17. In the changed kernel itself it should cost little, because VectorE is full beside it; it is a part of what makes the repair (e5) fail. No run has all three ties undone.

What the change is worth at best is an estimate from e17: 109.64 + 105.00 us of a full TensorE at 1.00 from 131 us on, and 5.6 for the stacks, would put A at 351, 7 us ahead of the kernel before. No run shows it, and VectorE, at work until 374 in e17 with the counts and masks that it took over there, would have to be rid of them. VectorE's 38.8 us of sums were paid for with nearly as much on an engine that was itself busy for 194 of 227 us.
